# Two groups of a feed-forward chunk by eight block products instead of seven

## The chip, the cores and the metric

One Trainium2 chip, of which the kernel uses one core. The metric is the device time of one execution in microseconds (us). The kernel is measured as the median of several runs; beside them one execution is taken with the hardware profiler, and every duration below comes from that one.

## The reference, cut to what matters

One layer of a hybrid encoder block over 256 tokens and 2048 features in float32. Three branches (a gated linear recurrence, attention with a forget gate, multi-scale pooling) are merged by sigmoid gates and go through an output projection with a residual. The change lies in what follows it, the feed-forward:

```python
x = x + merged @ w_out                       # 2048 x 2048
h2 = rms_norm(x, g_ffn)
gate, up = jnp.split(h2 @ w_ffn_in, 2, axis=-1)   # 2048 x (2 * 5632)
x = x + (jax.nn.silu(gate) * up) @ w_ffn_out      # 5632 x 2048
return rms_norm(x, g_final)
```

## The kernel before, in words

Every weight arrives in float32 by a 1 MB transfer into a raw buffer and is split into two parts: `whi`, a rounded cast on ACT, and `wlo`, the rest, a subtraction on DVE. A product is the sum of three matmuls on such parts. Out-projection and feed-forward follow each other without a break on PE: the output projection makes 16 blocks of the residual `xt` in turn (`m` from 0 to 15), and each block is at once turned into operands of the feed-forward (`hs`, seven forms a block).

**Forms.** Write x(f, t) for the scaled residual of feature half f (blocks 0 to 7, 8 to 15) and token half t. Form 0 is x(1,1) and form 4 is x(1,1) - x(1,2): both need only blocks 0 to 7. Forms 1, 2, 3, 5 and 6 need blocks 8 to 15 too, so the last one, `m` = 15, has to be there before they can be used.

**Groups.** The first feed-forward matrix is worked through in 22 groups. A group takes four weight blocks (`b11` and `x` of the first feature half for gate and up, `b21` and `b22` of the second) and makes gate and up for 256 hidden features. `group` (from L774) does it with seven block products by a Strassen-like scheme. For that it needs weight sums: `x` is loaded with the block `b22` added on the way (`load_sum`, a second transfer by POOL's queue, L674), `q2` adds `b11` to it (DVE, L777), `q4` adds the result to `b21` by a transfer from buffer to buffer (POOL's queue, L788), `q1` subtracts `b22` (DVE, L791). `plain` does it with the eight products of the ordinary block scheme and no weight sums: each block is split once and serves two products. `PLAIN` lists the groups that go by `plain`; it is empty here.

**Pieces.** Each block product comes in two pieces: one half of a weight block (128x1024) is cast and subtracted, and PE runs 12 matmuls of 128x256 with it (8 on `whi`, 4 on `wlo`). In `plain` a piece feeds 24 matmuls. A group by `group` is 14 pieces, a group by `plain` 8. `run` splits up to three pieces ahead (`LOOK`), and there are four pairs of `whi` and `wlo`: the split of a piece waits until PE has finished the piece four places before. PSUM has four tiles (`bank`) for the sums.

**Order.** `first(nxt)` puts the first product of the next group into the middle of a group. The statistics of the second norm (`stats`, L885) run behind an early product of group 0. `turn` transposes a finished group's result behind a later product of the next one (four small matmuls, L831). Each chunk of four groups is followed by its part of the second matrix (`down`, the tiles `obank`, L96 to L98), whose pieces are put into the four `slot`s of the next chunk's groups. Chunk 0, groups 0 to 3, has no such pieces beside it.

**Transfers.** Seven raw buffers serve the feed-forward. A buffer that comes free takes the next load in the list of `todo`, ordered by first use; the loads are issued on SP's queue in the order of the program, so a load that waits for its buffer keeps back all that follow it. The sums by POOL's queue stand in order on that queue too. Pools and a scheduler with priorities set the order of the instructions of each engine; `split_piece` raises the priority of the first splits.

Of the kernel before, what the change touches and what calls it, by code (L numbers as in the profile page):

```python
# [7 lines left out]
F32 = mybir.dt.float32  # L8
# [4 lines left out]
P = 128  # L13
T = 256
# [14 lines left out]
GATES = (2, 2, 2, 4)  # L29
CHUNKS = (4, 4, 4, 4, 4, 2)  # L30
SLOTS = (1, 1, 1, 1, 1, 2)
PLAIN = ()
LOOK = 3
LEAD = 8
RAW2 = 4
# [9 lines left out]
def block_kernel(ctx: ExitStack, tc: tile.TileContext, xT, vec,  # L45
                 wvf, wqk, wxy, wpi, wgate, wri, wpool, wbr, wout, wffi, wffo, out):
    nc = tc.nc
    V, S, G, PE = nc.vector, nc.scalar, nc.gpsimd, nc.tensor
# [5 lines left out]
    sm = ctx.enter_context(tc.tile_pool(name="sm", bufs=2))  # L54
# [29 lines left out]
    def mm_t(ps, hi, lo, rhs, nk, first, last):  # L84
        for k in range(nk):
            w = slice(k * P, (k + 1) * P)
            PE.matmul(ps, lhsT=hi[:, w], rhs=rhs(k), start=first and k == 0, stop=False)  # L87
            PE.matmul(ps[:, :T], lhsT=lo[:, w], rhs=rhs(k)[:, :T], start=False,  # L88
                      stop=last and k == nk - 1)
# [122 lines left out]
    for o, v, first in ((LF, -1.0, 64), (RF, 1.0, 0)):  # L212
        G.memset(o.bitcast(F32), 0.0)
        for base in (-first, -first - 32):
            G.affine_select(out=o, in_=o, compare_op=ALU.not_equal, fill=v, base=base,
                            pattern=[[-1, H], [0, T]], channel_multiplier=1)
# [443 lines left out]
    def halves(r):  # L660
        return r.rearrange("p (j c) -> p j c", j=2)
# [5 lines left out]
    class Group:  # L667
        def __init__(self, i):
            def load(s, h):
                return lambda r: nc.sync.dma_start(halves(r), block(i, s, h))  # L670
# [6 lines left out]
            self.b11 = Weights(load(0, 0))  # L677
            if i in PLAIN:
                self.x = Weights(load(1, 0))
# [10 lines left out]
    def product(g, w, form, c, start, pre=None, done=None, post=None, more=()):  # L690

        for h in range(2):
            def mm(hi, lo, h=h):
                o = g.place(c)
                for part, v in ((0, hi), (1, hi), (0, lo)):
                    for j in range(4):
                        PE.matmul(o, lhsT=hs[:, 4 * h + j, form, part, :], rhs=v[:, :, j * P:(j + 1) * P],  # L697
                                  start=start and h == 0 and part == 0 and v is hi and j == 0,
                                  stop=h == 1 and v is lo and j == 3, skip_group_check=True)

            Piece(lambda h=h: halves(w.tile)[:, :, h * 512:(h + 1) * 512], mm, [w, *more],
                  [pre] if pre and h == 0 else [], [done] if done and h else [],
                  [post] if post and h else [])

    def tmp(nm):
        return ft_p.tile([P, T], F32, name=nm)

    def gated(t, a, up, g):

        V.scalar_tensor_tensor(a, up, r2[:, t:t + 1], g, ALU.mult, ALU.mult)  # L710
# [3 lines left out]

    def first(g):
        if g.i in PLAIN:
            both(g, g.b11, (("A", 0, True), ("C", 4, True)), lambda: copy(g, "m1", "A"))
        else:
            product(g, g.b11, 0, "A", True, post=lambda: copy(g, "m1", "A"))

    def copy(g, name, c):
        g.m1 = tmp(name)
        S.copy(g.m1, g.bank[c])

    def both(g, w, todo_, post):

        for h in range(2):
            def mm(hi, lo, h=h):
                for c, form, start in todo_:
                    o = g.place(c)  # L730
                    for part, v in ((0, hi), (1, hi), (0, lo)):
                        for j in range(4):
                            PE.matmul(o, lhsT=hs[:, 4 * h + j, form, part, :],
                                      rhs=v[:, :, j * P:(j + 1) * P],
                                      start=start and h == 0 and part == 0 and v is hi and j == 0,
                                      stop=h == 1 and v is lo and j == 3, skip_group_check=True)

            Piece(lambda h=h: halves(w.tile)[:, :, h * 512:(h + 1) * 512], mm, [w], [], [],
                  [post] if h else [])

    def plain(g, nxt, slot, mid):

        def half(c):
            t = sm.tile([P, T], F32, name="t0" if c == "" else "evt")
            V.tensor_sub(t, g.m1, g.bank["C" + c])
            return t

        def gates():
            g.g0 = sm.tile([P, T], F32, name="t1")
            S.activation(g.g0, g.bank["A"], AF.Silu, scale=r2[:, 0:1])  # L750
            g.d = half("")
            V.tensor_add(g.d, g.d, g.bank["B"])
            S.activation(g.d, g.d, AF.Silu, scale=r2[:, 1:2])

        def ups():
            u = half("u")
            g.u1 = tmp("u1")
            V.tensor_add(g.u1, u, g.bank["Bu"])
            gated(1, g.u1, g.u1, g.d)
            g.m1 = tmp("m1")  # L760
            gated(0, g.m1, g.bank["Au"], g.g0)

        mid()
        slot(0)
        both(g, g.b21, (("A", 1, False), ("B", 2, True)), gates)
        slot(1)
        both(g, g.x, (("Au", 0, True), ("Cu", 4, True)), lambda: copy(g, "m1", "Au"))
        slot(2)
        if nxt is not None:
            first(nxt)  # L770
        both(g, g.b22, (("Au", 1, False), ("Bu", 2, True)), ups)
        slot(3)

    def group(g, nxt, slot, mid):  # L774
# [48 lines left out]
    def turn(g, c, f):  # L823

        if f == 0:
            acts[c] = act_p.tile([P, 2 * max(CHUNKS), 2 * T], F32R, name="act")
        act = acts[c]
        tp = aux_p.tile([P, 2, T], F32, name="turn")
        for j in range(2):
            for t, a in enumerate((g.m1, g.u1)):  # L830
                PE.transpose(tp[:, j, t * P:(t + 1) * P], a[:, j * P:(j + 1) * P], ident.bitcast(F32))  # L831
        S.copy(act[:, f:f + 2, :T], tp)  # L832
        V.tensor_sub(act[:, f:f + 2, T:], tp, act[:, f:f + 2, :T].bitcast(F32))  # L833
# [42 lines left out]
    def behind(f):  # L876

        line[-1].post.append(f)
# [14 lines left out]
    for i, (c, at) in enumerate(owner):  # L893
        g, prev = nxt, (g if i else None)
        nxt = Group(i + 1) if i + 1 < len(owner) else None

        def slot(k):
            n = SLOTS[c] if c < len(SLOTS) else 1
            if nxt is None and k == 3:
                return  # L900
            for _ in range(n):
                if queue:
                    queue.pop(0)()

        def mid():
            if prev is None:
                behind(stats)
                return
            pc, pat = owner[i - 1]
            behind(lambda a=(prev, pc, 2 * pat): turn(*a))  # L910
            if pc != c:
                queue.extend(down(pc))

        (plain if i in PLAIN else group)(g, nxt, slot, mid)
    while queue:
# [13 lines left out]
    for m in range(KD):  # L929
# [4 lines left out]
        with tc.high_priority(offset=AHEAD):  # L934
            V.tensor_add(xt[:, m, :], xt[:, m, :], o)
            hm = scaled(m, "hm", 2)
            if m < KB:
                c = hg_p.tile([P, 1, P], F32, name="hd")
# [3 lines left out]
            else:  # L942
                h0 = scaled(k, "h0", 1)
                c = hg_p.tile([P, 3, P], F32, name="hc")
# [114 lines left out]
```

## Time and profile before

| | us |
|---|---|
| median of 3 runs | 1558.33 (1556.02 to 1559.73) |
| profiled execution, its own time | 1557.26 |
| its span, first to last instruction | 1555.6 |
| PE (matmul) busy | 1517.7, 98% |
| PEld (weight loads) busy | 1418.4, 91% |
| DVE busy | 1244.9, 80% |
| ACT busy | 939.4, 60% |
| POOL busy | 161.4, 10% |
| first feed-forward matmul (L697) starts | 817.67 |
| first matmul of the second matrix (L96) starts | 935.96 |

A page of the profile gives the busy time of each engine and, for matmuls, their modelled ends: they are pipelined, so a busy PE isn't PE at its peak, and what counts on PE is the distance from one start to the next. A timeline row gives the start, the time of the whole row (the last instruction included), the engine, the line, what is written and read, how many instructions are merged, and in brackets how long the engine sat idle before and who released it. PEclk is the granted share of TensorE's clock: 1.00 is the upper of its two levels, 2.4 GHz, and 0.50 would be the lower.

### The profile page before, as it was taken

Reading aid. Unit: us, or ns where it says so; the run is one execution under the profiler, and the core shown is the slowest. Engines: PE = TensorE matmul, PEld = TensorE weight load, DVE = VectorE, ACT = ScalarE, POOL = GpSimd, SP = SyncE. Lnnn points to the kernel's source line nnn. Section 1 sums busy time; section 2 is a strip of 40 time slices with the busy share of each in tenths; the row PEclk is TensorE's granted clock in tenths of the full one; section 3 lists DMA queues with packets and bytes.
Section 4 is the critical chain, followed back from the end, with each engine's and each line's share of the span. In section 5 each row is a group of like instructions: output and inputs, shape, how many; then the busy total and the mean of one; then the engine's idle time right before and its main releaser. Section 6 shows DMA issues by size and latency. Waiting matters only on the chain.

```text
span 1555.6 us, 26488 instructions
## 1 busy us (share of the span) xinstructions
PE 1517.7 (98%) x10578; PEld 1418.4 (91%) x10578; DVE 1244.9 (80%) x1602; ACT 939.4 (60%) x1333; POOL 161.4 (10%) x210
## 2 busy tenths in 40 slices
PE   7999999999999999999998999999999999999996
PEld 7888888888888888888888989999999999999996
DVE  9876677887655656567799999999998999999875
ACT  6665566766444444445676656666666666666555
POOL 7400011011000000000111000000000000000003
PEclk8999999999999999999999899999999999999998
DMA  7544455555555555556865889898888979987761
GB/s 247 173 156 159 142 173 193 203 180 181 188 203 170 200 188 188 198 168 228 292 211 156 234 246 253 282 290 247 241 262 277 295 233 263 295 277 243 244 190 55
DMA packets 73276, 335.30 MB, mean 216 GB/s; under 512 B 5824, under 2 KB 8640, under 8 KB 54976
## 3 DMA queue, kind: packets, MB, share of 16 engines
q1 hardware_dynamic: 63424, 286.54, 51.3%
q0 software_dynamic: 9152, 46.14, 15.9%
q8 instruction: 83, 1.36, 0.3%
q10 hardware_dynamic: 576, 0.92, 0.2%
q14 instruction: 41, 0.34, 0.1%
HBM read 308.41 MB, written 2.10 MB: 200 GB/s over the span
## 4 chain that ended last, share of the span: by engine, by line
PE 86%; DVE 5%; issue 3%; POOL 2%; DMA 2%; ACT 2%; POOLq 0%; DVEq 0%; ACTq 0%
PE acc L87 29%; PE bank L697 25%; PE acc L88 15%; PE obank L98 5%; PE obank L96 5%; PE obank L97 5%; DVE wlo L639 2%; DMA raw<-in_wffi 1%; ACT whi L638 1%; POOL xn L238 1%; POOL part L150 1%; PE turn L831 1%; DMA raw<-raw 1%; DVE raw L791 1%; DVE raw L777 0%
## 5 line engine op out<-in xcount | busy, mean ns | idle before, releaser
L638 ACT CAST whi<-raw 128x1024 fp32r<-128x1024 f32 x396 | 409.2, 1050 | 253.1 <-PE obank L97 86.9
L639 DVE TENSOR_TENSOR wlo<-raw,whi 128x1024 fp32r<-128x1024 f32 x396 | 470.0, 1218 | 40.8 <-ACT whi L638 37.9
L75 DVE TENSOR_TENSOR wlo<-raw,whi 128x1024 fp32r<-128x1024 f32 (+3 forms) x282 | 346.8, 1232 | 190.8 <-ACT whi L74 189.9
L87 PE MATMUL acc<-hT,whi 128*128 128x512 f32 x1392 | 490.2, 395 | 0.0
L74 ACT CAST whi<-raw 128x1024 fp32r<-128x1024 f32 (+3 forms) x282 | 289.3, 1028 | 217.1 <-PE acc L87 181.1
L88 PE MATMUL acc<-hT,wlo 128*128 128x256 f32 x1392 | 390.7, 281 | 0.0
L697 PE MATMUL bank<-whi,hs 128*128 128x256 f32 x2464 | 352.1, 285 | 9.7 <-ACT whi L638 9.7
L697 PEld LDWEIGHTS bank<-whi,hs 128*128 128x128 f32 x2464 | 319.6, 192 | 12.0 <-ACT whi L638 11.7
L87 PEld LDWEIGHTS acc<-hT,whi 128*128 128x128 f32 x1392 | 261.6, 188 | 59.7 <-DVE vhl L290 0.2
L88 PEld LDWEIGHTS acc<-hT,wlo 128*128 128x128 f32 x1392 | 262.0, 188 | 0.2
L697 PE MATMUL bank<-wlo,hs 128*128 128x256 f32 x1232 | 199.0, 284 | 2.6 <-DVE wlo L639 2.6
L98 PE MATMUL obank<-act,wlo 128*128 128x256 f32 x704 | 197.6, 281 | 0.9 <-DVE wlo L639 0.9
L96 PE MATMUL obank<-act,whi 128*128 128x256 f32 x704 | 197.8, 281 | 0.0
L97 PE MATMUL obank<-act,whi 128*128 128x256 f32 x704 | 197.1, 280 | 0.5 <-DVE act L833 0.5
L697 PEld LDWEIGHTS bank<-wlo,hs 128*128 128x128 f32 x1232 | 170.6, 192 | 3.0 <-DVE wlo L639 3.0
L97 PEld LDWEIGHTS obank<-act,whi 128*128 128x128 f32 x704 | 132.9, 189 | 0.7 <-DVE act L833 0.7
L98 PEld LDWEIGHTS obank<-act,wlo 128*128 128x128 f32 x704 | 132.4, 188 | 1.3 <-DVE wlo L639 1.3
L96 PEld LDWEIGHTS obank<-act,whi 128*128 128x128 f32 x704 | 132.4, 188 | 0.6 <-ACT act L832 0.2
L87 PE MATMUL acc<-mT,whi 128*128 128x512 f32 x256 | 90.0, 396 | 0.0
L674 POOL DMA_DIRECT2D raw<-in_wffi x22 | 26.6, 1210 | 488.2 <-DMA raw<-in_wffi 244.7
L88 PE MATMUL acc<-mT,wlo 128*128 128x256 f32 x256 | 71.7, 281 | 0.0
L856 DVE TENSOR_TENSOR xt<-xt,obank 128x256 f32<-128x256 f32 x96 | 39.9, 416 | 26.1 <-PE obank L98 26.1
(272 smaller groups left out, 1705.7 us busy)
## 6 DMA issues: line engine op xcount, KB each, us to landing
raw<-in_wffi SPq DMA_DIRECT2D x88, 1024.0 KB, 7.2
raw<-in_wgate SPq DMA_DIRECT2D x48, 1024.0 KB, 4.9
raw<-in_wffo SPq DMA_DIRECT2D x44, 1024.0 KB, 8.3
raw<-in_wffi POOLq DMA_DIRECT2D x22, 1024.0 KB, 8.5
raw<-raw POOLq DMA_DIRECT2D x22, 1024.0 KB, 9.1
raw<-in_wqk SPq DMA_DIRECT2D x16, 1024.0 KB, 4.8
raw<-in_wxy SPq DMA_DIRECT2D x16, 1024.0 KB, 4.8
raw<-in_wbr SPq DMA_DIRECT2D x16, 1024.0 KB, 5.0
```

Source lines behind the costliest of these rows:

```text
L74: S.copy(hi[:, :n], r[:, a:a + n])
L75: V.tensor_sub(lo[:, :n], r[:, a:a + n], hi[:, :n].bitcast(F32))
L87: PE.matmul(ps, lhsT=hi[:, w], rhs=rhs(k), start=first and k == 0, stop=False)
L88: PE.matmul(ps[:, :T], lhsT=lo[:, w], rhs=rhs(k)[:, :T], start=False, stop=last and k == nk - 1)
L96: PE.matmul(o, lhsT=hi[:, w], rhs=rhs(k)[:, :T], start=first and k == 0, stop=False)
L97: PE.matmul(o, lhsT=hi[:, w], rhs=rhs(k)[:, T:], start=False, stop=False)
L98: PE.matmul(o, lhsT=lo[:, w], rhs=rhs(k)[:, :T], start=False, stop=last and k == nk - 1)
L638: S.copy(hi, w)
L639: V.tensor_sub(lo, w, hi.bitcast(F32))
L674: G.dma_start(halves(r), block(i, 1, 1), accum_op=ALU.add)
L697: PE.matmul(o, lhsT=hs[:, 4 * h + j, form, part, :], rhs=v[:, :, j * P:(j + 1) * P], start=start and h == 0 and part == 0 and v is hi and ...
L856: V.tensor_add(xt[:, m, :], xt[:, m, :], ps)
```

## The change

Groups 0 and 2 go by `plain`. The bodies of `first` and `plain` are changed with it: the first two block products of a group now use forms 0 and 4 on `b11`, the next two forms 0 and 4 on `x`, and only then come `b21` and `b22` with forms 1 and 2. The subtraction that frees the bank of form 4 stands directly behind its product (`less`). A group by `plain` issues no sums on POOL's queue and no `q1` and `q2`.

```diff
-PLAIN = ()
+PLAIN = (0, 2)
...
     def first(g):
         if g.i in PLAIN:
-            both(g, g.b11, (("A", 0, True), ("C", 4, True)), lambda: copy(g, "m1", "A"))
+            both(g, g.b11, (("C", 4, True), ("A", 0, True)), lambda: less(g, "t0", "A", "C"))
         else:
             product(g, g.b11, 0, "A", True, post=lambda: copy(g, "m1", "A"))
+
+    def less(g, name, a, c):
+
+        copy(g, "m1", a)
+        g.t = sm.tile([P, T], F32, name=name)
+        V.tensor_sub(g.t, g.m1, g.bank[c])
...
-        def half(c):
-            t = sm.tile([P, T], F32, name="t0" if c == "" else "evt")
-            V.tensor_sub(t, g.m1, g.bank["C" + c])
-            return t
+        def up_less():
+            g.d = g.t
+            less(g, "evt", "Au", "Cu")
...
-            g.d = half("")
             V.tensor_add(g.d, g.d, g.bank["B"])
...
-            u = half("u")
             g.u1 = tmp("u1")
-            V.tensor_add(g.u1, u, g.bank["Bu"])
+            V.tensor_add(g.u1, g.t, g.bank["Bu"])
...
+        slot(0)
+        both(g, g.x, (("Cu", 4, True), ("Au", 0, True)), up_less)
         mid()
-        slot(0)
-        both(g, g.b21, (("A", 1, False), ("B", 2, True)), gates)
         slot(1)
-        both(g, g.x, (("Au", 0, True), ("Cu", 4, True)), lambda: copy(g, "m1", "Au"))
+        both(g, g.b21, (("B", 2, True), ("A", 1, False)), gates)
         slot(2)
         if nxt is not None:
             first(nxt)
-        both(g, g.b22, (("Au", 1, False), ("Bu", 2, True)), ups)
+        both(g, g.b22, (("Bu", 2, True), ("Au", 1, False)), ups)
```

PE, the start of the feed-forward, before (a bank is one block product's sum, a `whi` one piece; `turn` is the statistics):

```order
L697 MATMUL bank_8237<-whi_8221,hs_7185 128x256 x8
L697 MATMUL bank_8237<-wlo_8222,hs_7185 128x256 x4
L697 MATMUL bank_8237<-whi_8225,hs_7185 128x256 x8
L697 MATMUL bank_8237<-wlo_8226,hs_7185 128x256 x4
L697 MATMUL bank_8273<-whi_8229,hs_7185 128x256 x8
L697 MATMUL bank_8273<-wlo_8230,hs_7185 128x256 x4
L697 MATMUL bank_8273<-whi_8233,hs_7185 128x256 x8
L697 MATMUL bank_8273<-wlo_8234,hs_7185 128x256 x4
L697 MATMUL bank_8307<-whi_8251,hs_7185 128x256 x8
```

The same place in the changed kernel, the first two of its first four pieces (the other two, on 8229 and 8233, are alike), and what follows them:

```order
L739 MATMUL bank_8238<-whi_8220,hs_7185 128x256 x8
L739 MATMUL bank_8238<-wlo_8221,hs_7185 128x256 x4
L739 MATMUL bank_8251<-whi_8220,hs_7185 128x256 x8
L739 MATMUL bank_8251<-wlo_8221,hs_7185 128x256 x4
L739 MATMUL bank_8238<-whi_8224,hs_7185 128x256 x8
L739 MATMUL bank_8238<-wlo_8225,hs_7185 128x256 x4
L739 MATMUL bank_8251<-whi_8224,hs_7185 128x256 x8
L739 MATMUL bank_8251<-wlo_8225,hs_7185 128x256 x4
...
L888 MATMUL turn_8359<-ones_94,sacc_7197 128x1
```

Four pieces stand before the first late form (on `whi_8251` before, on `whi_8264` behind the statistics now) in both; they are 48 matmuls before and 96 now.

DVE, the end of the output projection, before (`t0` and `xt` are block 15 of the residual, `hc` and `hs` its forms, L777 is `q2` and L791 is `q1` of group 0):

```order
L106 TENSOR_TENSOR t0_8171<-acc_8128,evt_8172 128x256
L777 TENSOR_TENSOR raw20_7189<-raw20_7189,raw21_7190 128x2048
L935 TENSOR_TENSOR xt_77<-xt_77,t0_8171 128x256
L791 TENSOR_TENSOR raw21_7190<-raw20_7189,raw23_7192 128x2048
L945 TENSOR_TENSOR hc_8180<-h0_8178,hm_8176 128x128
L597 TENSOR_TENSOR hs_7185<-hm_8176,hs_7185 128x2x128
L946 TENSOR_TENSOR hc_8180<-h0_8178,hc_8180 128x128
L639 TENSOR_TENSOR wlo_8252<-raw20_7189,whi_8251 128x1024
L947 TENSOR_TENSOR hc_8180<-hm_8176,hc_8180 128x128
L597 TENSOR_TENSOR hs_7185<-hc_8180,hs_7185 128x128
L639 TENSOR_TENSOR wlo_8270<-raw20_7189,whi_8269 128x1024
L597 TENSOR_TENSOR hs_7185<-hc_8180,hs_7185 128x2x128
```

The same place in the changed kernel:

```order
L106 TENSOR_TENSOR t0_8171<-acc_8128,evt_8172 128x256
L938 TENSOR_TENSOR xt_77<-xt_77,t0_8171 128x256
L948 TENSOR_TENSOR hc_8180<-h0_8178,hm_8176 128x128
L949 TENSOR_TENSOR hc_8180<-h0_8178,hc_8180 128x128
L950 TENSOR_TENSOR hc_8180<-hm_8176,hc_8180 128x128
L597 TENSOR_TENSOR hs_7185<-hm_8176,hs_7185 128x2x128
L597 TENSOR_TENSOR hs_7185<-hc_8180,hs_7185 128x128
L597 TENSOR_TENSOR hs_7185<-hc_8180,hs_7185 128x2x128
L639 TENSOR_TENSOR wlo_8265<-raw23_7192,whi_8264 128x1024
L639 TENSOR_TENSOR wlo_8297<-raw23_7192,whi_8296 128x1024
```

The forms of block 15 stand right behind it now, with no weight sum and no split between them.

DVE, the passage into group 3, before (L777 and L791 are `q2` and `q1` of group 3, L710 and L804 the end of group 2):

```order
L639 TENSOR_TENSOR wlo_9014<-raw_8212,whi_9013 128x1024
L710 SCALAR_TENSOR_TENSOR m1_8719<-m1_8719,r2_7196,t1_8904 128x256
L777 TENSOR_TENSOR raw_8212<-raw_8212,raw21_7190 128x2048
L804 TENSOR_TENSOR t0_8860<-t0_8860,bank_8796 128x256
L791 TENSOR_TENSOR raw21_7190<-raw_8212,raw23_7192 128x2048
L639 TENSOR_TENSOR wlo_9031<-raw_8212,whi_9030 128x1024
```

The same place in the changed kernel (L780 is `q2`, L794 is `q1`, L761 and L710 are the end of group 2):

```order
L639 TENSOR_TENSOR wlo_8989<-raw_8213,whi_8988 128x1024
L780 TENSOR_TENSOR raw_8213<-raw_8213,raw22_7191 128x2048
L794 TENSOR_TENSOR raw22_7191<-raw_8213,raw_8214 128x2048
L639 TENSOR_TENSOR wlo_9019<-raw_8213,whi_9018 128x1024
L761 TENSOR_TENSOR u1_9046<-evt_8882,bank_8992 128x256
L710 SCALAR_TENSOR_TENSOR m1_9049<-bank_8839,r2_7196,t1_8948 128x256
L710 SCALAR_TENSOR_TENSOR u1_9046<-u1_9046,r2_7196,t0_8747 128x256
```

Both weight sums of group 3 now stand ahead of the end of group 2, which waits for PE; before, they stood behind parts of it.

## Rows read from the trace of the kernel before

**Rows 1.** The page: busy time of each engine, and the group of casts.

```profile
PE 1517.7 (98%) x10578; PEld 1418.4 (91%) x10578; DVE 1244.9 (80%) x1602; ACT 939.4 (60%) x1333; POOL 161.4 (10%) x210
...
L638 ACT CAST whi<-raw 128x1024 fp32r<-128x1024 f32 x396 | 409.2, 1050 | 253.1 <-PE obank L97 86.9
```

**Rows 2.** Busy time by stretch: start:end, length, busy by engine, PEclk, DMA share, GB/s.

```profile
817.67:850.62 32.95, 29.25 (x222) 28.83 (x221) 30.06 (x44) 21.50 (x30) 3.39 (x4) 0.90 0.50 150
850.62:875.52 24.90, 22.44 (x174) 22.01 (x173) 23.55 (x25) 15.41 (x18) 2.10 (x2) 0.93 0.89 249
875.52:901.56 26.04, 23.60 (x174) 23.16 (x173) 24.87 (x27) 16.73 (x19) 2.10 (x2) 0.87 0.91 253
901.56:923.87 22.31, 21.20 (x175) 20.57 (x173) 21.08 (x23) 14.61 (x18) 0.90 (x1) 1.00 0.90 250
923.87:935.96 12.09, 9.50 (x54) 8.97 (x53) 11.92 (x12) 8.08 (x10) 2.11 (x2) 0.72 0.65 158
...
1040.00:1240.00 200.00, 200.00 (x1696) 200.00 (x1695) 185.33 (x203) 127.63 (x140) 12.69 (x12) 1.00 0.87 268
```

**Rows 3.** Who released PE between 817 and 936: us in total, times, longest.

```profile
PE bank L697 <- ACT whi L638: 9.7, 8, 2.4
PE bank L697 <- DVE wlo L639: 2.6, 1, 2.6
```

**Rows 4.** Timeline of PE at the start of the feed-forward.

```profile
817.67 1.11 PE L697 MATMUL bank<-whi,hs 128*128 128x256 f32 x8
...
824.60 1.21 PE L697 MATMUL bank<-whi,hs 128*128 128x256 f32 x8 [1.10 <-ACT whi L638]
828.41 1.22 PE L697 MATMUL bank<-wlo,hs 128*128 128x256 f32 x4 [2.60 <-DVE wlo L639]
```

**Rows 5.** Timeline of PE, a dense stretch, and the first matmul of the second matrix.

```profile
893.00 1.10 PE L697 MATMUL bank<-whi,hs 128*128 128x256 f32 x8
...
901.56 0.27 PE L831 MATMUL turn<-ident,m 128*128 128x128 f32 x1
901.84 1.21 PE L697 MATMUL bank<-whi,hs 128*128 128x256 f32 x8
...
935.96 0.28 PE L96 MATMUL obank<-act,whi 128*128 128x256 f32 x1
```

**Rows 6.** Timeline of DVE while block 15 becomes forms.

```profile
820.79 0.42 DVE L106 TENSOR_TENSOR t<-acc,evt 128x256 f32<-128x256 f32 x1
...
823.33 0.42 DVE L935 TENSOR_TENSOR xt<-xt,t 128x256 f32<-128x256 f32 x1
...
825.87 0.82 DVE L945 TENSOR_TENSOR hc<-h,hm 128x128 f32<-128x128 f32 x1
...
829.82 0.41 DVE L597 TENSOR_TENSOR hs<-hc,hs 128x256 fp32r<-128x256 f32 x1
```

**Rows 7.** Timeline of DVE: what each of its operations takes in a row.

```profile
855.04 4.62 DVE L639 TENSOR_TENSOR wlo<-raw,whi 128x1024 fp32r<-128x1024 f32 x4
859.58 0.41 DVE L781 TENSOR_TENSOR t<-m,bank 128x256 f32<-128x256 f32 x1
859.91 0.68 DVE L833 TENSOR_TENSOR act<-turn,act 128x512 fp32r<-128x512 f32 x1
...
922.61 0.48 DVE L710 SCALAR_TENSOR_TENSOR m<-m,r,t 128x256 f32<-128x256 f32 x1
923.01 2.29 DVE L777 TENSOR_TENSOR raw<-raw,raw 128x2048 f32<-128x2048 f32 x1
925.21 0.41 DVE L804 TENSOR_TENSOR t<-t,bank 128x256 f32<-128x256 f32 x1
```

**Rows 8.** Transfers from 760 to 960 us: issues, KB, median us to landing; then three POOL issues, 870 to 900.

```profile
raw<-in_wffi SPq DMA_DIRECT2D x22, 1024.0 KB, 7.0
...
raw<-raw POOLq DMA_DIRECT2D x5, 1024.0 KB, 8.2
...
DMA to landing us min/median/max: 7.9/11.1/11.1
```

## The prediction

> **What bounds the kernel now.** I began with the page: PE is busy for 98% of the span, its weight loads for 91%, DVE for 80% [rows 1]. Taken over the whole span that says PE, and a change that adds matmuls should cost. But the share is an average, so I cut the place of the change into stretches, from the first feed-forward matmul at 817.67 to the first matmul of the second matrix at 935.96. The cuts are the first transpose of each group's `turn`. From 1040 on PE has no gap and DVE is below it (185.3 of 200). In the five stretches of chunk 0 it is the other way round: DVE is busy for 0.91, 0.95, 0.96, 0.94 and 0.99 of the time, weight loads for 0.88, 0.88, 0.89, 0.92 and 0.74, and the granted clock falls to between 0.72 and 0.93 in four of the five [rows 2]. So the reader should see two regimes: DVE-bound in chunk 0, PE-bound behind it.
>
> How much does PE lose there? In a dense stretch six pieces, 893.00 to 901.56, start 8.56 us apart in all, so 1.427 us for a piece of 12 matmuls, 0.119 for one [rows 5]. Chunk 0 and the start of group 4 are 18, 14, 14, 14 and 4 pieces between the cuts, 64 in all, worth 91.3 us of the 118.3 [rows 2, 5]. The losses by stretch are 7.3, 4.9, 6.1, 2.3 and 6.4, in sum 27.0 us. Some 2.4 of these are the 16 transposes and four small matmuls of the statistics (an estimate: 20 places of 0.119), which stay. Idle time that the waits show is 9.7 us on casts and 2.6 on subtractions [rows 3]; the rest is matmuls at the lower clock behind such gaps.
>
> **The change part by part.**
>
> Added on PE: groups 0 and 2 become eight products, 192 matmuls instead of 168. That is 48 matmuls, four pieces' worth: +5.7 us, all of it on PE, where nothing hides it.
>
> Removed on DVE: in a row a subtraction takes 1.135 us (4.54 for four), a weight sum 2.20, a 128x256 operation 0.33, a gated one 0.40, and the split of `act` 0.68 [rows 7]. A group by `group` is 14 x 1.135 + 2 x 2.20 + 5 x 0.33 + 2 x 0.40 + 0.68 = 23.4 us on DVE against 14 x 1.427 = 20.0 on PE. A group by `plain` is 8 x 1.135 + 4 x 0.33 + 2 x 0.40 + 0.68 = 11.9 on DVE against 16 x 1.427 = 22.8 on PE. So DVE loses 11.5 us of work in each of two groups, and the order within chunk 0 alternates between PE-bound and DVE-bound groups. The casts on ACT fall from 14 to 8 a group and two transfers a group vanish from POOL's queue; neither was the bound, so I book nothing for them.
>
> Start of group 0. Before, PE has four pieces (5.7 us, 817.67 to 823.4) that need no late form, then waits 1.1 and 2.6 us [rows 4]; block 15's forms end on DVE only at 830.2, because `q2`, `q1` and two splits stand between [rows 6]. Now the four early pieces are 96 matmuls, 11.4 us, to 829.1. On DVE `q2` no longer stands between 820.79 and xt of block 15, which is done at about 821.5 instead of 823.7. From xt to the last form took 6.5 us, 823.7 to 830.2 [rows 6], with `q1` and two splits inside, 4.5 us [rows 7]; that leaves 2.0, and I take 2.7 because an activation that `q1` covered now stands bare. Forms at 824.2, first late split at 825.4; with all 6.5 us it would be 828. Margin 3.7 us, so the whole loss of the first stretch goes. What is late next there: the sum for `g.d` and two Silu activations, which follow the product that PE ends at 835.2 and free a bank that PE wants at 838.1, when group 1's first product is through; they have 2.9 us for three short instructions.
>
> Group 1 (by `group`) between two plain ones. Walking the new order with these durations: PE reaches its first piece at 843.7. DVE is ahead: `q2` runs 840.9 to 843.1, beside group 0's last pieces, and the split behind it stands at 846.1, PE asks at 846.6. `q1` runs 849.5 to 851.7, its split stands at 853.8, PE asks at 853.8. So the loss of 4.9 shrinks to its transposes and about 0.3, but with margins between 0 and 0.5 us. These are the thinnest of the chunk, and if they fail the 4.5 us above the transposes come back.
>
> `q4` of group 1, a transfer on POOL's queue, now issues at about 849.6 behind the added load for group 3. It is wanted split at 864.2; a cast and a subtraction take 1.05 and 1.14 [rows 1, 7], so it must land by 862. With 8.2 it lands at 858, with 11.1, the longest of three, at 860.7 [rows 8]. SP's queue stands behind it: its next entry reloads the buffer that `q4` reads, and the load of group 2's `b21` is queued after that. With 860 and 7.0 for a load [rows 8] it is there at 867 to 868 and needed by 871. I book nothing, 3 us of cover.
>
> Sums on POOL's queue have a page price too. The Trainium skill, DMA: Bandwidth & Descriptors, section Anatomy of one DMA, fits such a transfer as 2.0 us plus bytes over 436 GB/s, 4.4 us for 1 MB. This trace measures 7.9 to 11.1, so the measurement is used; by the page's price group 3's `q4` would come early enough to gain about 1.4 us more than I forecast.
>
> Group 2 (plain) needs 11.9 of 22.8 us on DVE; its loss goes down to the transposes. In DVE's slack the scheduler puts both weight sums of group 3, at about 884 to 889, ahead of the end of group 2.
>
> So from 817.67 to the piece that uses `q2` of group 3, PE is dense but for 0.3 us: 600 matmuls as 50 x 1.427 (71.35), 12 small ones at 0.119 (1.4), together 73.1, at 890.75. Before, the same piece starts at 901.84 [rows 5]. **Gain to there: 11.1 us**, the 5.7 already paid.
>
> Group 3 is DVE-bound again. Before, from this piece to `q2` of group 4 at 923.01 [rows 7] took 21.2 us. Now 2.2 of it (`q1`) is done beforehand. What may come late is its own `q4`: by my walk it issues at 894.4 and lands 8.2 to 11.1 us later [rows 8], at 902.6 to 905.5. The split behind it is otherwise free at about 902, and what follows on DVE puts `q2` of group 4 at 908.7 to 911.7, 18.0 to 21.0 us after the piece. **Gain here 0.2 to 3.2, taken 2.4**: near the end of the median landing of `raw<-raw`, with 0.8 off for the hops between engines, which the walk counts as nothing. From `q2` of group 4 the order is that of before, 12.95 us to 935.96, its gaps included, and from there on PE had no gap to give.
>
> Sum: 11.1 + 2.4 = 13.5 us. The profiled execution's own time was 1557.26, so 1543.8 for it; it ran 1.07 under the median of 1558.33, which gives **1544.8** for the median.
>
> **The rivals.**
>
> *No gap left.* If group 3 and the start of group 4 were dense as well, all 27.0 - 2.4 go and 5.7 come: 18.9 us, 1539.4. For: DVE's work from 817.67 on falls below PE's. Against: `q2`, `q1` and the gated operations stand in one row of DVE before group 4 in both orders, and that row made the last 6.4 us.
>
> *The thin margins of group 1 fail*, or its `q4` lands late: 4.5 us stay, 1549.3. For: a margin of 0 to 0.5 us by durations without the time from one engine to the next. Against: DVE enters group 1 ahead by a `q2`.
>
> *PE is the bound and the losses stay.* The mechanism: four pairs of `whi` and `wlo`. A plain piece holds its pair for 2.85 us instead of 1.43, so ACT and DVE cannot run further ahead than now, the slack of plain groups is lost, and groups 1 and 3 pay as before; then block 15 only moves the wait. 5.7 us are added: 1564.0. It decides once more than 27.0 - 5.7 = 21.3 us of loss remain between the two marks. Against it: in group 1 three pieces of cover are enough for one weight sum, and the first stretch's 7.3 vanish by the order of DVE alone. The Trainium skill, Perfetto Trace Analysis, section Identifying the Most-Contended Engine, judges the tensor engine by its weight loads; by that rule over the whole span PE (91%) stands before DVE (80%), and 48 more matmuls cost 5.7. The trace agrees from 1040 on, and by stretch it disagrees in chunk 0, which the same page allows for (several regimes).
>
> *It does nothing that lasts*: the gain of chunk 0 is taken back in chunk 1 because loads then come late. For: DMA engines are busy 0.87 there. Against: PE waits for nothing. 1558.
>
> **How the numbers follow.** Forecast 13.5: 0.60. No gap left: 0.12. Thin margins: 0.18. PE bound, slower: 0.05. Nothing that lasts: 0.05. 0.2% is 3.1 us, about what a measurement here can tell. Faster by more: 0.60 + 0.12 + 0.18 = 0.90; within: 0.05; slower: 0.05. The range takes in the dense case and the thin margins with 1.5 us of the runs' own spread: 1538.5 to 1551.
>
> **What would show it.** Right: no gap on PE at the first late piece; forms of block 15 before 825; the granted clock at 1.00 from 817 to the passage into group 4; the first `obank` matmul at 921 to 924. Wrong: idle time before the pieces behind `q2` and `q1` in group 1, a cast that waits for `raw<-raw`, or the old length of 21 us in group 3; then the forecast falls to the second or third rival.

## The result and the profile after

The changed kernel takes 1541.65 us (median of 4 runs, 1540.54 to 1546.28) against 1559.03 for the kernel before, measured beside it on the same chip. The ratio is 0.990, with a 95% interval of 0.9883 to 0.9917: faster by 1.0%. The forecast was 1544.8 with a range of 1538.5 to 1551, so sign and range hold; the time came out 3.1 us under the forecast. The profiled execution took 1542.72 us, its span is 1541.0, against 1557.26 and 1555.6.

The page first, busy time of each engine and the group of casts, to lay beside [rows 1]:

```profile
PE 1514.3 (98%) x10626; PEld 1416.2 (92%) x10626; DVE 1222.6 (79%) x1584; ACT 928.9 (60%) x1323; POOL 155.5 (10%) x206
...
L638 ACT CAST whi<-raw 128x1024 fp32r<-128x1024 f32 x384 | 396.8, 1050 | 240.0 <-PE obank L97 94.6
```

PE has its 48 matmuls more, DVE 22.3 us less to do (forecast: 23.0), ACT 12 casts less. The shares have hardly moved; whoever reads only this part sees no reason for a gain of 1%. The stretches show it. These are the windows of the kernel after, cut as in [rows 2] (first matmul of the feed-forward, first transpose of each group's `turn`, first matmul of the second matrix); columns are start:end, length, busy time of PE, PEld, DVE, ACT and POOL, PEclk, DMA share, GB/s:

```profile
818.60:850.30 31.70, 31.70 (x271) 31.70 (x270) 25.57 (x42) 20.40 (x30) 2.18 (x3) 1.00 0.49 143
850.30:873.98 23.68, 23.63 (x199) 23.35 (x198) 20.54 (x23) 15.12 (x18) 0.90 (x1) 1.00 0.90 295
873.98:894.29 20.31, 20.31 (x175) 20.31 (x174) 16.65 (x17) 12.15 (x16) 1.19 (x1) 1.00 0.65 195
894.29:911.82 17.53, 17.53 (x150) 17.53 (x149) 16.47 (x18) 9.99 (x12) 0.89 (x1) 1.00 0.86 268
911.82:920.99 9.17, 6.66 (x54) 6.22 (x53) 9.17 (x10) 8.00 (x10) 2.09 (x2) 1.00 0.57 130
1040.00:1240.00 200.00, 200.00 (x1695) 200.00 (x1695) 187.69 (x204) 128.75 (x140) 14.73 (x14) 1.00 0.87 260
```

In the first four windows PE and its weight loads are now busy from end to end (23.63 and 23.35 of 23.68 us in the second), DVE is busy for 0.81, 0.87, 0.82 and 0.94 of them, and the granted clock is 1.00 in all. The regime of DVE is gone from chunk 0 except for the passage into group 4, the fifth window, where DVE is busy for all of 9.17 us and PE for 6.66. From the first window's start to the last cut it took 118.29 us, now 102.39: 15.9 us less, with 48 matmuls more in it. From 1040 on PE is busy without a gap, as before.

Who released PE, in the same stretch (800 to 935; in us total, times, longest), beside [rows 3]:

```profile
PE bank L697 <- ACT whi L638: 2.5, 2, 1.4
```

Of 12.3 us of waiting 2.5 are left, and the timeline of PE shows where they are, as [rows 4] and [rows 5] did before (start, duration, operation, idle time before it and its releaser):

```profile
818.60 1.11 PE L739 MATMUL bank<-whi,hs 128*128 128x256 f32 x8
...
830.34 1.16 PE L739 MATMUL bank<-whi,hs 128*128 128x256 f32 x8
...
891.42 1.10 PE L697 MATMUL bank<-whi,hs 128*128 128x256 f32 x8
...
911.82 0.27 PE L834 MATMUL turn<-ident,m 128*128 128x128 f32 x1
913.52 1.21 PE L697 MATMUL bank<-whi,hs 128*128 128x256 f32 x8 [1.42 <-ACT whi L638]
915.81 0.74 PE L697 MATMUL bank<-whi,hs 128*128 128x256 f32 x4 [1.09 <-ACT whi L638]
916.39 0.63 PE L697 MATMUL bank<-wlo,hs 128*128 128x256 f32 x4
...
920.99 0.28 PE L96 MATMUL obank<-act,whi 128*128 128x256 f32 x1
```

830.34 is the first piece that needs block 15; no idle time stands before it. The next idle time of PE is the 1.42 us before 913.52.

### The profile page after: what moved, and what is told of

Read it like the earlier page. It is cut to its first block, busy times and chain, and to the rows that moved or that the text cites. A ratio compares the mean times of both kernels' runs of the same rounds, so it can differ in the third digit from the quotient of the medians.

```text
span 1541.0 us, 26532 instructions
## 1 busy us (share of the span) xinstructions
PE 1514.3 (98%) x10626; PEld 1416.2 (92%) x10626; DVE 1222.6 (79%) x1584; ACT 928.9 (60%) x1323; POOL 155.5 (10%) x206
## 4 chain that ended last, share of the span: by engine, by line
PE 86%; DVE 5%; issue 3%; DMA 2%; POOL 2%; ACT 1%; SPq 0%; POOLq 0%; DVEq 0%; ACTq 0%
PE acc L87 30%; PE bank L697 21%; PE acc L88 15%; PE obank L98 5%; PE obank L96 5%; PE obank L97 5%; PE bank L739 3%; DVE wlo L639 2%; DMA raw<-raw 1%; DMA raw<-in_wffi 1%; POOL xn L238 1%; POOL part L150 1%; ACT whi L638 1%; PE turn L834 1%; DVE raw L780 0%
## 5 line engine op out<-in xcount | busy, mean ns | idle before, releaser
L638 ACT CAST whi<-raw 128x1024 fp32r<-128x1024 f32 x384 | 396.8, 1050 | 240.0 <-PE obank L97 94.6
L639 DVE TENSOR_TENSOR wlo<-raw,whi 128x1024 fp32r<-128x1024 f32 x384 | 456.6, 1220 | 44.7 <-ACT whi L638 44.0
L697 PE MATMUL bank<-whi,hs 128*128 128x256 f32 x2240 | 312.8, 282 | 2.5 <-ACT whi L638 2.5
L697 PEld LDWEIGHTS bank<-whi,hs 128*128 128x128 f32 x2240 | 284.6, 188 | 3.0 <-ACT whi L638 3.0
L697 PE MATMUL bank<-wlo,hs 128*128 128x256 f32 x1120 | 178.1, 281 | 0.8 <-DVE wlo L639 0.6
L697 PEld LDWEIGHTS bank<-wlo,hs 128*128 128x128 f32 x1120 | 152.1, 188 | 1.4 <-DVE wlo L639 1.4
L674 POOL DMA_DIRECT2D raw<-in_wffi x20 | 24.2, 1211 | 474.0 <-DMA raw<-in_wffi 233.2
```

The lines of the kernel that those rows point to most:

```text
L638: S.copy(hi, w)
L639: V.tensor_sub(lo, w, hi.bitcast(F32))
```

## The experiments

The theory put to the test is that of the prediction: DVE was the bound in chunk 0 and PE behind it, and a group in the new form leaves DVE some 11 us of slack in which it runs ahead into the next. The rivals are that the order of the products did it, that each microsecond off DVE counts for itself, that the transfers which vanish from POOL's queue did it, and that only the number of groups counts. "Chunk 0" below is the length between the two outer cuts (118.29 before, 102.39 changed); each median stands against the median of the kernel before measured beside it. Those medians differ (1558.06 for e0 to e3, 1556.98 for e4 to e7, 1557.37 for e8 to e10), so a distance of about 1 us from the changed kernel's 1541.62 is not resolved.

**The changed kernel once more** (`e0_again`).

> The changed kernel once more, as the mark for the others on this chip. Theory A (chunk 0 was bound by DVE and by the late forms): 14 to 17 us under the kernel before. Open point: in its first profile the passage into group 4, from q2 of group 4 to the first obank matmul, took 10.97 us instead of 12.95 because the granted clock stayed at 1.00. If that belongs to the kernel, it is 11.0 again (within 0.3); if it is chance, it may be 13 with a clock near 0.7 there.

Measured: 1541.62 against 1558.06, ratio 0.9891 [0.9874, 0.9907]; chunk 0 took 102.46. The profile repeats to 0.1 us there, and the open point is answered: from `q2` of group 4 (909.95) to the first `obank` matmul (920.91) it took 10.96 us again, with a granted clock of 1.00, so this belongs to the kernel.

**Each group alone** (`e1_only_group0`, `e2_only_group2`).

```diff
-PLAIN = (0, 2)
+PLAIN = (0,)      # e1;  (2,) in e2
```

> Group 0 alone by eight products, group 2 by seven as before. Theory A: the first stretch loses its 7 us and group 1 about 3 of its 4.5, 2.85 us of matmuls come, groups 2 and 3 and the passage into group 4 are as before: 7 us under the kernel before (5 to 9), PE dense up to group 1 and gaps again at the weight sums of groups 2, 3 and 4. Rival B (PE is the bound): 2.85 us over it. Rival C (all of the gain is the start of group 0, group 2 does nothing): 13 to 17 under it.

> Group 2 alone by eight products, group 0 by seven as before. Theory A: the gaps of the first stretch and of group 1 stay, those of group 2, group 3 and half of the passage into group 4 go (6.1 + 1.9 + 2, less 0.9 of transposes), 2.85 us come: 6.5 us under the kernel before (4 to 9). Rival B: 2.85 over it. Rival C: 0 to 3 over it. If A holds, the gains of this and of group 0 alone add up to that of both within 3 us.

Measured: group 0 alone 1553.41 against 1558.06, 4.65 us less, ratio 0.9968 [0.9956, 0.998]; group 2 alone 1554.39, 3.7 less, 0.9981 [0.9966, 0.9995]. Both gain, neither as much as expected. In chunk 0 they do what was expected, 111.39 and 112.17 us, so 6.9 and 6.1 less. What group 0 alone loses again lies far behind: from the first to the last matmul of the second matrix its profiled execution takes 609.33 us instead of 606.31. In e1 the timelines of ACT and then of PE show a late load:

```profile
1462.04 2.00 ACT L638 CAST whi<-raw 128x1024 fp32r<-128x1024 f32 x2 [5.74 <-DMA raw<-in_wffi]
```

```profile
1468.89 0.36 PE L96 MATMUL obank<-act,whi 128*128 128x256 f32 x1 [1.96 <-DVE xt L859]
```

Between 1450 and 1490 PE of the kernel before waits 0.9 us in all, none of it on `xt`. That the late load caused the wait is argued from the order of the two rows, not shown. The one stretch of one execution also varies: it took 606.73 and 605.06 us in two executions of the changed kernel. The six runs of e1 lie close together (1552.28 to 1554.72, the profiled one 1553.85), so its smaller gain is no accident of one execution, but what costs it in the others is not known. For group 2 alone there is no such loss (606.47 us); its profiled run was its fastest, 1551.90, and its ten runs spread to 1561.75, so the median stays under what chunk 0 gave.

The two gains in chunk 0 sum to 13.0, both groups together give 15.9. The missing 2.9 us are the passage into group 4: 12.41 and 12.02 us alone, 12.09 before, 9.17 with both.

**The old order of the eight products** (`e3_old_order`): the kernel before with one line changed.

```diff
-PLAIN = ()
+PLAIN = (0, 2)
```

> Groups 0 and 2 by eight products, but in the order of the unused code of the kernel before: b11 with forms 0 and 4, then b21 with the late forms 1 and 2, then x. Theory A: only two pieces, 48 matmuls or 5.7 us, need no late form, so PE comes to the late piece at about 824.3 and finds its split at about 827: a gap of 2 to 4 us at the start of group 0 and a lower clock behind it, else as the changed kernel; 3 to 5 us over the changed kernel, 11 to 13 under the kernel before. Rival D (the order is worth nothing, the eight products do it all): within 1 us of the changed kernel.

Measured: 1542.53 against 1558.06, ratio 0.9906 [0.9883, 0.9929], only 0.9 us above the changed kernel. Chunk 0 took 103.72, 1.3 more. The expectation (3 to 5) was too high by a factor of three; the rival by which the eight products do it all held. Timeline of PE in e3, the only wait before the passage:

```profile
826.16 1.21 PE L733 MATMUL bank<-whi,hs 128*128 128x256 f32 x8 [1.20 <-ACT m L723]
```

The wait is there, at the first late piece, but the forms of block 15 are early in this kernel too, since `q1` and `q2` of group 0 no longer stand between them on DVE; and the eight matmuls behind the wait take 1.21 us, no longer than behind other waits at the upper clock. What ends the wait is the copy of a bank on ACT (`m`), not the split that the expectation named. So the order in which the change puts the blocks is worth about 1 us; the eight products bring the rest.

**Two more groups where PE is the bound** (`e4_late_groups`).

```diff
-PLAIN = (0, 2)
+PLAIN = (0, 2, 10, 14)
```

> Groups 10 and 14, in chunks 2 and 3, also by eight products. Theory A: PE is the bound there, so 2 x 24 more matmuls at 0.119 us cost 5.7 us over the changed kernel (4.5 to 7), the busy time of DVE falls and nobody gains by it. Rival E (DVE is close enough to the bound everywhere, 93% from 1040 on, that a plain group helps anywhere): the same as the changed kernel or faster.

Measured: 1546.62 against 1556.98, ratio 0.9929 [0.9914, 0.9943]: 10.4 us under the kernel before, and 5.0 above the 1541.62 of the changed kernel (expected 5.7, 4.5 to 7). The window 1040 to 1240 of e4:

```profile
1040.00:1240.00 200.00, 200.00 (x1696) 200.00 (x1695) 167.63 (x187) 117.60 (x129) 10.46 (x10) 1.00 0.81 252
```

DVE does 20.1 us less than in the changed kernel, and PE and its weight loads are busy for 200 of 200 in both. Where PE has no gap, the same edit costs the time of its matmuls. Here the Trainium skill, Perfetto Trace Analysis, section Identifying the Most-Contended Engine, which judges TensorE by its weight loads, agrees with the run; chunk 0 is where the rule over the whole span misled.

**All of chunk 0** (`e5_all_of_chunk0`), **and groups 0, 2 and 4** (`e9_groups_0_2_4`).

```diff
-PLAIN = (0, 2)
+PLAIN = (0, 1, 2, 3)      # e5;  (0, 2, 4) in e9
```

> Groups 0, 1, 2 and 3 by eight products. Theory A: 5.7 us of matmuls come, and of the gaps only the 3 us before the first obank matmul are left to go: 2.7 to 5.7 us over the changed kernel, 10 to 13 under the kernel before. Rival E: faster than the changed kernel by 2 us or more.

> Groups 0, 2 and 4 by eight products, to take away the last gap, 3.5 us at the weight sums of group 4. Theory A: 2.85 us of matmuls come and the passage becomes dense: between 0.7 us faster and 1.5 us slower than the changed kernel, so no gain worth having. Rival E: 2 us faster or more.

Measured: 1542.53 against 1556.98, 0.9907 [0.9891, 0.9922], and 1542.02 against 1557.37, 0.9895 [0.9872, 0.9918]. In both PE waits for nothing at all between 815 and 925. With all four groups chunk 0 takes 104.57 us, 2.2 more than in the changed kernel: 5.7 of matmuls come, the passage's two waits of 2.5 in sum go, and the remaining 1.0 was not taken apart. In the median it is 0.9 more, where 2.7 to 5.7 were expected: a miss. The expectation had counted 3 us of the passage as given back, so that is not its reason, which stays open. With group 4 the last cut comes at 99.23, 3.2 us earlier, but the median is the same: the 24 matmuls that group 4 has more, 2.9 us, lie behind that cut. The changed kernel has little left to win here; what a further group saves in waiting it pays in matmuls.

**Work put back on DVE** (`e6_two_idle_sums`, `e7_six_idle_sums`): operations of the size of a weight sum, each the maximum of a block with itself, ahead of the last block's split in groups 0 and 2.

```diff
+        def idle(w, n):
+            def f():
+                for _ in range(n):
+                    V.tensor_max(w.tile, w.tile, w.tile)
+            return f
...
-        both(g, g.b22, (("Bu", 2, True), ("Au", 1, False)), ups)
+        both(g, g.b22, (("Bu", 2, True), ("Au", 1, False)), ups, pre=idle(g.b22, 2))   # 6 in e7
```

> The changed kernel with two idle weight sums on DVE in each of groups 0 and 2: the maximum of b22's buffer with itself, 128x2048, ahead of the split of b22 (the result is unchanged). That gives DVE back 4.5 us in each plain group, as much as q1 and q2 took. Theory A: a plain group has 11 us of slack on DVE, so this is hidden: at most 1 us over the changed kernel. Rival F (what counts is DVE's work as such): 9 us over it.

> The same with six idle sums in each of groups 0 and 2, 13.4 us of DVE each, more than the slack of 11 us, and in one row where the pieces split ahead cover 6 to 8 us of PE. Theory A: PE waits 5 to 8 us in each of the two groups, with a lower clock behind the gap: 9 to 18 us over the changed kernel, a bend against the two sums. Rival F: in proportion, three times what two sums cost, 27 us if those cost 9.

Measured: with two, 1542.90 against 1556.98, 0.9904 [0.9888, 0.9921], 1.3 us above the changed kernel; with six, 1558.01, 1.0009 [0.9997, 1.0021], 16.4 above it, so the whole gain is gone. Chunk 0 took 105.16 and 119.36, 2.8 and 17.0 more than in the changed kernel. DVE did not run all of these operations inside the groups they were meant for. The timelines of DVE and of PE in e6 (L769 is an idle sum):

```profile
810.23 2.28 DVE L769 TENSOR_TENSOR raw<-raw 128x2048 f32<-128x2048 f32 x1
...
813.90 2.29 DVE L769 TENSOR_TENSOR raw<-raw 128x2048 f32<-128x2048 f32 x1
...
871.44 2.29 DVE L769 TENSOR_TENSOR raw<-raw 128x2048 f32<-128x2048 f32 x1
...
874.77 2.29 DVE L769 TENSOR_TENSOR raw<-raw 128x2048 f32<-128x2048 f32 x1
```

```profile
830.88 1.21 PE L739 MATMUL bank<-whi,hs 128*128 128x256 f32 x8 [0.97 <-DVE t L725]
```

The two sums of group 0 ran in the output projection, before the feed-forward began at 818.01. There they put DVE back: the forms of block 15 end at 827.6 instead of 825.4, PE waits 0.97 us, and the first stretch takes 32.90 us instead of 31.70. The two sums of group 2 are the test that was meant: the three stretches from 850.91 to 912.42 take 23.67, 20.31 and 17.53 us, as in the changed kernel to 0.01. So 4.6 us more on DVE in a group in the new form are hidden, where a cost by each microsecond would show all of them. The other 1.6 us of the 2.8 lie in the passage into group 4 (last section). In e7 two sums of group 0 lie ahead of the feed-forward too, four in it, and all six of group 2, 13.7 us, in that group. They are not hidden: PE waits 6.0 us behind three of them in one row (expected 5 to 8), while group 0's wait of 2.8 is less than expected. So a bend is shown for group 2, between 4.6 us that are hidden and 13.7 that are not; the 11 us of slack in the theory lie between, and no run measures their size. Past it the old picture is back: who released PE in e7 between 815 and 940 (us in total, times, longest), and a window of its start:

```profile
PE bank L739 <- ACT whi L638: 6.0, 1, 6.0
PE bank L697 <- ACT whi L638: 4.1, 3, 1.7
PE bank L739 <- DVE t L725: 2.8, 1, 2.8
```

```profile
818.00:850.00 32.00, 29.23 (x226) 29.15 (x226) 29.84 (x42) 17.73 (x30) 1.96 (x3) 0.89 0.40 132
```

DVE is busy for 0.93 of that window, the granted clock is down to 0.89, beside 0.90 in the first line of [rows 2].

**Groups 0 and 3** (`e8_groups_0_and_3`): the same number of groups in the new form, but two in the old form in a row between them.

```diff
-PLAIN = (0, 2)
+PLAIN = (0, 3)
```

> Groups 0 and 3 by eight products, so groups 1 and 2 by seven follow each other. Theory A (each plain group hides the weight sums of the group behind it, one group by seven is carried, a second in a row is not): the gap at the weight sums of group 2 comes back, about 5.6 us, and the passage into group 4 becomes dense, 3.5 us less: from the first feed-forward matmul to the first obank matmul 104 to 105 us instead of 102.4, 1 to 3 us over the changed kernel. Rival G (only the number of plain groups counts): within 0.7 us of it.

Measured: 1540.53 against 1557.37, ratio 0.9888 [0.9869, 0.9908]: 1 us below the changed kernel and not to be told from it, where 1 to 3 more were expected. Chunk 0 took 102.26 (expected 104 to 105). The timeline of PE shows that the second old group in a row does wait, behind its two weight sums, and PE waits nowhere else in chunk 0:

```profile
869.46 1.20 PE L697 MATMUL bank<-whi,hs 128*128 128x256 f32 x8 [1.08 <-ACT whi L638]
871.76 0.74 PE L697 MATMUL bank<-whi,hs 128*128 128x256 f32 x4 [1.09 <-ACT whi L638]
```

So the pattern moves the one place where DVE's lead runs out from group 4 to group 2, and the cost is alike, some 2.2 us of waiting. The 5.6 us expected there were the old loss with its lower clock; the granted clock of group 2's stretch was 1.00 here. That new and old groups must alternate is refuted; the rival by which the number of groups counts held.

**The two sums back on POOL's queue** (`e10_pool_sums_back`): block `x` of groups 0 and 2 is fetched with `b22` added to it, as before the change. The products of those groups then use this sum instead of the block.

```diff
-                self.x = Weights(load(1, 0))
+                self.x = Weights(load_sum, LEAD)
```

> The changed kernel, but x of groups 0 and 2 is loaded with b22 added by POOL's queue and eight pieces ahead, as in a group by seven; the products then take this sum for x, so the result is not the reference's. This puts two of the four transfers back that the change took off POOL's queue, and the DVE order nearly as it is. Theory A (DVE and the late forms were the bound, the transfers were not): within 1.5 us of the changed kernel. Rival H (the freed transfers made the gain): 5 us or more over it, casts waiting for raw<-in_wffi.

Measured: 1541.77 against 1557.37, ratio 0.9897 [0.9877, 0.9917]; chunk 0 took 102.48. So the two sums on loading were not the bound; the one of group 0 runs at 738 us, far ahead of chunk 0, the one of group 2 at 826.19. The other two transfers that the change removed, the `q4` of groups 0 and 2, were not put back.

**A rival that no run tested.** Each group in the new form also takes six casts off ACT, and 9.7 of the 12.3 us for which PE waited ended with a cast [rows 3]. The trace of the kernel before speaks against ACT as the cause: it is busy for 0.62 to 0.67 of the five stretches [rows 2], and four of its casts there waited 17.3 us in all for a weight sum on DVE. The cast that releases PE at 926.51, in its timeline of ACT:

```profile
925.41 1.05 ACT L638 CAST whi<-raw 128x1024 fp32r<-128x1024 f32 x1 [4.59 <-DVE raw L777]
```

## Why the prediction was right, and the one term that was too small

**Start of group 0.** Forecast: forms of block 15 at 824.2, margin 3.7 us, no wait. The feed-forward itself began 0.93 us later in the profiled execution (818.60 against 817.67; the profiled executions of the eleven experiments lie between these two), so the forecast reads 825.1 here, and the sign "before 825" reads 825.9. The timeline of DVE has the last form ending at 825.43, beside 830.2 in [rows 6]:

```profile
824.79 0.64 DVE L597 TENSOR_TENSOR hs<-hc,hs 128x128 fp32r<-128x128 f32 x2
...
841.72 2.29 DVE L780 TENSOR_TENSOR raw<-raw,raw 128x2048 f32<-128x2048 f32 x1
...
850.14 2.29 DVE L794 TENSOR_TENSOR raw<-raw,raw 128x2048 f32<-128x2048 f32 x1
...
885.00 2.29 DVE L780 TENSOR_TENSOR raw<-raw,raw 128x2048 f32<-128x2048 f32 x1
887.33 2.29 DVE L794 TENSOR_TENSOR raw<-raw 128x2048 f32<-128x2048 f32 x1
...
910.02 2.28 DVE L780 TENSOR_TENSOR raw<-raw,raw 128x2048 f32<-128x2048 f32 x1
```

What the prediction did not take apart is how much of this is the order and how much the missing sums; e3 says 1.3 us for the order.

**Group 1.** `q2` and `q1` were forecast at 840.9 and 849.5, with the shift 841.8 and 850.4; they stand at 841.72 and 850.14. The thin margins held: no wait of PE in that window. The second rival (0.18) would have left 4.5 us.

**Group 3's transfer.** Forecast: `q4` issues at 894.4 (895.3 with the shift) and lands 8.2 to 11.1 us later. The timelines of POOL and of ACT:

```profile
850.53 0.90 POOL L791 DMA_DIRECT2D raw<-raw  x1 [4.66 <-DVE wlo L639]
...
895.58 0.89 POOL L791 DMA_DIRECT2D raw<-raw  x1 [15.84 <-DVE wlo L639]
```

```profile
903.67 2.00 ACT L638 CAST whi<-raw 128x1024 fp32r<-128x1024 f32 x2 [2.45 <-DMA raw<-raw]
```

The cast that had waited 2.45 us for it starts 8.09 us behind the issue, just below the short end of the forecast. The long end, 11.1, was a misreading: of the three issues in [rows 8] the two with 11.1 are sums on loading (L674), and the five transfers from buffer to buffer between 760 and 960 us landed after 7.9 to 9.8 us. The Trainium skill, DMA: Bandwidth & Descriptors, section Anatomy of one DMA, gives an estimate of 4.4 us; the measurement disagrees again, and decides. A cast that waits for `raw<-raw` was among the prediction's signs of being wrong, and this one did wait; PE did not, so the sign was badly chosen.

**To the piece with `q2` of group 3.** Forecast 73.1 us after the start; it starts at 891.42, which is 72.8. The gain to there is 11.3 us instead of 11.1. Group 3's weight sums stand at 885.00 and 887.33, where 884 to 889 was forecast. From the piece to `q2` of group 4 the forecast was 18.8 us, measured 18.6 (891.42 to 910.02): a gain of 2.6 instead of 2.4.

**From `q2` of group 4 to the first matmul of the second matrix** the prediction wrote "the order is that of before, 12.95 us to 935.96, its gaps included". It took 10.97 us (910.02 to 920.99; the forecast sign for the end was 921 to 924). This is the term that was mis-sized, by 1.98 us. The kernel before has in its timeline of PE:

```profile
926.51 2.07 PE L697 MATMUL bank<-whi,hs 128*128 128x256 f32 x8 [2.37 <-ACT whi L638]
928.80 1.22 PE L697 MATMUL bank<-whi,hs 128*128 128x256 f32 x4 [0.22 <-ACT whi L638]
929.82 1.05 PE L697 MATMUL bank<-wlo,hs 128*128 128x256 f32 x4
```

The order is that of before, to the hundredth: the two pieces start 3.50 and 5.79 us after `q2` in both kernels (913.52 and 915.81 from 910.02; 926.51 and 928.80 from 923.01). So DVE's part was right. But eight matmuls behind the first gap took 2.07 us before and 1.21 now, and from the second piece to the first `obank` it took 7.16 us before and 5.18 now: all 1.98 us are matmuls at the lower of the clock's two levels. The granted clock of that window was 0.72 [rows 2], and is 1.00 now, in e0, e3, e4 and e10 too. The prediction carried over the length of a stretch, and with it its clock. The first gap is 0.95 us shorter because `q2` now starts 1.80 us ahead of the transposes at 911.82, instead of 0.86 ahead of those at 923.87.

**The sum.** In the traces 15.9 us were gained in chunk 0, forecast 13.5: 0.2, 0.2 and 2.0 of it are the three terms above. Of the 15.9 the execution gave back 0.93 by its later start and 0.42 behind the last cut (606.73 us from the first to the last matmul of the second matrix, 606.31 before), which leaves 14.55, and the profiled times differ by 14.54. Neither was forecast. The 0.42 is less than the 1.7 us by which two executions of the changed kernel differ in that stretch; the reason of the 0.93 is open. The rest of the 3.1 us between forecast and median is scatter: the profiled execution of before ran 1.07 under the median it was set against, that of after 1.07 over its own. So of the 3.1 us some 2 are scatter that happened to fall on the same side, and the median lies nearer to the rival without gaps (1539.4) than to the forecast; it is the trace that tells them apart. The low end of the stated range has 0.9 us of spread below that rival, not the 1.5 that the prediction names.

**The other rivals.** No gap left (1539.4) would have needed the passage to be dense as well; it is not, though it lost its low clock. PE as the bound (1564.0) decided above 21.3 us of remaining loss; 5.4 remain (102.39 less 68 pieces of 1.427), so it was far off, and e4 shows the place in which it is true. Nothing that lasts: refuted for the changed kernel; whether the loss of 3.0 us far behind in e1 has that mechanism is open.

## What to carry to other kernels

Choose between fewer products with sums and more products without them by stretch and not for the whole kernel. Here the extra matmuls paid for themselves where DVE, which makes the sums, was busy for over 0.9 of a stretch and PE had gaps and a granted clock below 1; where PE had no gap (e4, DVE busy for 0.94 before the edit) they cost nearly their full time. One relieved group also carried the next, because DVE kept its lead, so half of the groups were enough here, and more or other ones gained nothing measurable. When a stretch with waits is carried over from an old trace into a forecast, split it into what the chain of the other engine sets and what the clock makes of the matmuls behind it; only the first part stayed as it was here.

## What the runs showed of the hardware

The same passage into group 4 (48 matmuls of 256 columns, the same two waits on casts behind two weight sums) took between 9.1 and 12.4 us. Of the 2.9 us between before and changed 0.94 are the later start of the first piece (2.64 and 1.70 us behind the first transpose) and 1.98 the clock behind it. The timeline of PE in e6, where the clock fell late:

```profile
914.17 1.21 PE L697 MATMUL bank<-whi,hs 128*128 128x256 f32 x8 [1.47 <-ACT whi L638]
916.46 0.83 PE L697 MATMUL bank<-whi,hs 128*128 128x256 f32 x4 [1.08 <-ACT whi L638]
...
917.95 1.91 PE L697 MATMUL bank<-whi,hs 128*128 128x256 f32 x8
```

| kernel | idle before the two pieces, us | eight matmuls behind the first | passage, us |
|---|---|---|---|
| before | 2.37, 0.22 | 2.07 | 12.09 |
| group 2 alone | 2.40, 0.22 | 2.08 | 12.02 |
| group 0 alone | 2.21, 1.00 | 1.30 | 12.41 |
| six idle sums | 1.73, 1.08 | 1.21 | 10.85 |
| two idle sums | 1.47, 1.08 | 1.21 | 10.75 |
| changed | 1.42, 1.09 | 1.21 | 9.17 |
| old order | 1.34, 1.09 | 1.21 | 9.09 |

In this passage the shorter first idle times went with less of a fall, and with the changed kernel the clock stayed at its upper level, though two waits of over 1 us stand 2.3 us apart. The step from 1.42 to 1.47 us of idle time, with 1.6 us between the two passages, is too small to be the whole reason. Other places speak against idle time as the rule: in e1, 2.29 us ahead of a piece of group 3 left its eight matmuls at 1.21, and in the kernel before the clock fell at the same place of group 1 behind idle times shorter than the changed kernel's. Its timeline of PE:

```profile
852.26 1.21 PE L697 MATMUL bank<-whi,hs 128*128 128x256 f32 x8 [1.37 <-ACT whi L638]
854.56 1.08 PE L697 MATMUL bank<-whi,hs 128*128 128x256 f32 x4 [1.08 <-ACT whi L638]
```

Four matmuls take 1.08 us there and 0.74 in the changed kernel. What else the engine did before those gaps was not varied on its own, and what decides stays open. No version ran clearly below the changed kernel: groups 0 and 3 came 1 us lower, inside the spread.
